# A Strassen-Winograd feed-forward: six open steps in place of five, earlier sums and a deeper prefetch for the down projection

## The chip, the cores and the metric

One core of one Trainium2 chip runs the whole kernel. The metric is device time in microseconds (us); each figure for a kernel is the median of several runs, and the range of the runs stands beside it.

## What is computed

One decoder layer on 1024 tokens of width 1024, all in float32. Two attention groups run first; the change does not touch them. Then come the output projection with a residual and a layer norm, a SwiGLU feed-forward with a second norm, and a gated embedding with a third. Cut to what matters:

```python
mix = jnp.concatenate([o_nsa, o_mla], axis=-1) @ w_out[i]
x = _layer_norm(ALPHA * x + mix, ln1_g[i], ln1_b[i])
gu = x @ w_up[i]
ffn = (jax.nn.silu(gu[..., :D_FF]) * gu[..., D_FF:]) @ w_down[i]
x = _layer_norm(ALPHA * x + ffn, ln2_g[i], ln2_b[i])
```

D_FF is 2816, which is 22 tiles of 128.

## The kernel before

**Numbers.** A float32 operand is split into a high half in fp32r (`hi`, L103 to L107, mostly on ACT) and the rest (`lo`, L109 to L113, mostly on DVE). A product is then three matmuls (`mm3`, L120: high by high, high by low, low by high), so the low half of the stationary operand is first wanted by the third matmul, L124.

**Output projection.** The loop over the eight token blocks `tb` (L1193 on) runs `out_proj` (48 matmuls, residual, statistics of the norm), a scaling on ACT (L1213), and one turn later `x1_done` (gain on DVE, L914; bias on DVE, L918; a copy to DRAM, L1191) and `tr_x1` (eight transposes on PE, L989, copied out by ACT, L996). `t_sums` forms the Winograd combinations of the transposed activations and `put` splits them (L1017 on ACT, L1019 on DVE, four small instructions for two blocks).

**Gate and up.** Gate and up are computed with Winograd's seven products per step `i`, one step for each of the 22 tiles. `seq` lists the (step, product) pairs; `k` is the place in it. A product is twelve matmuls. The first products of a step, 1 and 2, need only the gate weights and two combinations that are ready early; the other five need sums of weights (`u_sum`, four POOL instructions, L1041 to L1045) and the later combinations. So the first `SKEW` steps are opened: their products 1 and 2 all come first in `seq` (ten products with `SKEW` at 5), and the rest follows. `u_split` splits weights; `"g"` is the gate half, `"s12"` and `"s34"` are the sums. `u_evac` takes results out of PSUM one product later (L1085 on ACT, L1090 on DVE, then Silu on ACT, L1091). `at_pos` hangs each of these jobs on a place `k`, and every engine runs its instructions in the order in which they were written: an instruction that waits holds up all that is behind it on its engine. SP issues all DMAs, in order too.

**Down.** `h_sums` (POOL) forms combinations of the hidden tile and stores them to DRAM; `units` are the 77 down products of twelve matmuls, each with one operand pair that `d_load` reads back (256 KB of hidden, 256 KB of weights) and `d_split` splits two units ahead. `d_load` runs four units ahead, because the tag `kk` has four buffers. At units 2 and 13 four residual blocks each (`x1d`, 512 KB) are loaded (L1340).

**Buffers.** `slot()` hands out 43 buffers of 4 KB per partition (tag `b`), `kslot()` four (tag `kk`), `hslot()` twelve of half the size (tag `h`).

Of the kernel before, what the change touches and what calls it, by code (L numbers as in the profile page):

```python
# [37 lines left out]
SKEW = 5  # L38
# [29 lines left out]
def body(tc, sb, dr, A, out, dbg, stop):  # L68
# [978 lines left out]
    def u_split(i, what):  # L1047
        if i >= NF:
            return
        if what == "u":  # L1050
            t = slot(F32R, T)
            h, l = t[:, :512], t[:, 512:]
            hi_lo(h, l, RAW[i][1][:, 512:])
            WP7[i, 4] = h, l
            return
        x = {"g": lambda: RAW[("g", i) if i < SKEW else i], "s12": lambda: SS[i, 0], "s34": lambda: SS[i, 1]}[what]()
        x = x[0] if what == "g" and i >= SKEW else x
        ps = {"g": (1, 2), "s12": (5, 6), "s34": (7, 3)}[what]
        h, l = slot(F32R, T), slot(F32R, T)
        hi_lo(h, l, x)  # L1060
        for n, c in zip(ps, (0, 512)):
            WP7[i, n] = h[:, c:c + 512], l[:, c:c + 512]
# [19 lines left out]
    def u_evac(i, n):  # L1082
        if n in (1, 6, 5):
            t = CO[i, n] = hslot()
            act.activation(t, BK[i, "x"], AF.Copy)  # L1085
            if n == 5:
                dve.tensor_add(t, t, BK[i, "z"])
        elif n == 2:
            t = CO[i, 1]
            dve.tensor_add(t, t, BK.pop((i, "y")))  # L1090
            act.activation(t, t, AF.Silu)  # L1091
        elif n == 3:
            t = hslot()
            act.activation(t, BK.pop((i, "x")), AF.Silu)
            h = CO.pop((i, 5))
            dve.tensor_mul(h, h, t)
            keep_h(i, 1, h)
        elif n == 4:
            h = CO.pop((i, 6))
            dve.tensor_add(h, h, BK.pop((i, "z")))  # L1100
            dve.tensor_mul(h, h, CO.pop((i, 1)))
            keep_h(i, 0, h)
# [7 lines left out]

    def h_sums(m):
        a11, a21, a12, a22 = HA.pop((2 * m, 0)), HA.pop((2 * m, 1)), HA.pop((2 * m + 1, 0)), HA.pop((2 * m + 1, 1))
        s1, s2 = hslot(), hslot()
# [46 lines left out]
    for i in range(NF):  # L1160
# [4 lines left out]
        at_pos(first - 6 if i else 1, u_sum, i, 0)  # L1165
        at_pos(first - 5 if i else 1, u_sum, i, 1)
# [13 lines left out]
    for k, nm, tbs in ((0, "t2", (6,)), (0, "t3", (4, 5)), (2, "t2", (7,)), (3, "t3", (6, 7)), (4, "t1", (4, 5)),  # L1180
                       (5, "t1", (6, 7)), (7, "22", (4, 5, 6, 7)), (10, "t4", (4, 5)), (11, "t4", (6, 7))):
        for tb in tbs:
            at_pos(k, put, tb, nm)
# [12 lines left out]
    for tb in range(NB):  # L1196
# [4 lines left out]
        if tb in (6, 7):  # L1201
            g_fetch(tb - 6)
        if tb:
            x1_done(tb - 1)
        if tb == 7:
            u_split(0, "g")
            u_split(1, "g")
            g_fetch(2)
            g_fetch(3)
        nrm = out_proj(tb)  # L1210
        if tb:
            tr_x1(tb - 1)
        act.activation(acc[tb], acc[tb], AF.Identity, scale=nrm[0], bias=nrm[1])  # L1213
        if 1 <= tb <= 4:
            put(tb - 1, "11")
            put(tb - 1, "21")
        elif tb:
            t_sums(tb - 1)
    WO = None
    u_fetch(0)  # L1220
    put(4, "t2")
    put(5, "t2")
# [9 lines left out]
    RW, UN = {}, {}  # L1232

    def d_load(k):
        if k < len(units):
            n, m = units[k]
            t = RW[k] = kslot(T, F32)
# [14 lines left out]
    for k, (i, n) in enumerate(seq):  # L1252
# [8 lines left out]
        if k in (1, 3, 5):  # L1261
            u_split(k // 2 + 2, "g")
        if k == 1:
            g_fetch(4)
        jobs(k)
        last = i, n
        if len(seq) - 6 <= k < len(seq) - 2:
            d_load(k - len(seq) + 6)
# [52 lines left out]
    XB, YB = {}, {}  # L1321
    for k, (n, m) in enumerate(units):
# [8 lines left out]
        d_load(k + 4)  # L1331
# [5 lines left out]
        if k in (2, 13):  # L1337
            for tb in range(k // 11 * 4, k // 11 * 4 + 4):
                acc[tb] = slot(n=D)
                nc.sync.dma_start(acc[tb], x1d[tb])  # L1340
# [155 lines left out]
```

## Time and profile before

| | |
|---|---|
| median of 3 runs | 1463.13 us (1462.27 to 1465.5) |
| the profiled execution | 1464.8 us, of it span 1463.0 us |
| PE busy | 1409.4 us, 96% of the span |
| PE weight loads busy | 1179.3 us, 81% |
| DVE busy | 1010.7 us, 69% |
| ACT busy | 709.9 us, 49% |
| POOL busy | 591.3 us, 40% |
| DMA | 159.85 MB, 109 GB/s on average |
| mean granted PE clock | 0.989 |

PE is the engine that does nearly all of the time, and its idle time sits in few places. The output projection ends, and gate and up begin, at about 677 us of the span; the down projection begins at about 1120 us. Matmuls of a run overlap in the records, so a record of 0.39 us in a run of equal matmuls stands for a step of less than that from start to start; losses are therefore better counted from starts than from the busy share.

### The profile page before, as it was taken

The page shows a single profiled execution, that of the slowest core. Times are in us where ns is not written, and L with a number is a line of the kernel's source. Part 1 is how long each engine was busy: PE and PEld are TensorE (multiplying, and loading weights), DVE is VectorE, ACT ScalarE, POOL GpSimd, SP SyncE. Part 2 cuts the span into 40 slices and gives each one's busy share as a digit, 9 for nine tenths or more (in the row PEclk, how much of TensorE's full clock was granted, in tenths as well). Part 3 has the DMA queues.
Part 4 walks back from the last instruction along what each step waited for, and adds up shares of the span by engine and source line. Part 5 has one row for each costly group of instructions (what it writes and reads, how often), then busy time and mean ns, then how long its engine had stood idle before and what let it go on. Part 6 is the DMA issues. An engine that isn't in the chain of part 4 may idle for free. (4 is left out here: it accounts for less than half of the span.)

```text
span 1463.0 us, 20518 instructions
## 1 busy us (share of the span) xinstructions
PE 1409.4 (96%) x7082; PEld 1179.3 (81%) x7082; DVE 1010.7 (69%) x1923; ACT 709.9 (49%) x1447; POOL 591.3 (40%) x570
## 2 busy tenths in 40 slices
PE   8999899999989999998899999999999999999997
PEld 8987778888768887887688788888877788888886
DVE  5367589999988998578755555555554565686775
ACT  3323499888888888233532333333232343333221
POOL 1321165545443338013366866666682011121332
PEclk9999999999999999999999999999999999999999
DMA  7031000000000014123145444444454887662001
GB/s 274 16 100 52 26 1 23 2 1 15 2 15 1 1 44 158 58 87 123 65 166 183 165 151 163 166 166 165 167 193 148 291 295 240 242 212 76 29 30 58
DMA packets 66488, 159.85 MB, mean 109 GB/s; under 512 B 8016, under 2 KB 8656, under 8 KB 66384
## 3 DMA queue, kind: packets, MB, share of 16 engines
q1 hardware_dynamic: 66384, 158.54, 31.2%
q8 instruction: 56, 0.92, 0.3%
q14 instruction: 48, 0.39, 0.1%
HBM read 118.40 MB, written 40.11 MB: 108 GB/s over the span
## 5 line engine op out<-in xcount | busy, mean ns | idle before, releaser
L122 PE MATMUL p<-b 128*128 128x512 f32 (+3 forms) x1524 | 585.1, 384 | 15.3 <-ACT b L105 10.3
L124 PE MATMUL p<-b 128*128 128x512 f32 (+3 forms) x1524 | 583.9, 383 | 3.3 <-DVE b L111 3.1
L123 PE MATMUL p<-b 128*128 128x512 f32 (+3 forms) x1524 | 581.9, 382 | 1.5 <-DVE b L111 1.5
L122 PEld LDWEIGHTS p<-b 128*128 128x128 f32 x1524 | 288.3, 189 | 70.9 <-ACT b L105 12.2
L124 PEld LDWEIGHTS p<-b 128*128 128x128 f32 x1524 | 288.2, 189 | 62.1 <-DVE b L111 8.8
L123 PEld LDWEIGHTS p<-b 128*128 128x128 f32 x1524 | 288.4, 189 | 53.5 <-DVE b L111 2.4
L111 DVE TENSOR_TENSOR b<-b 128x1024 fp32r<-128x1024 f32 (+4 forms) x162 | 204.0, 1277 | 173.4 <-ACT b L105 134.4
L111 DVE TENSOR_TENSOR h<-p,h 128x512 fp32r<-128x512 f32 (+1 forms) x244 | 148.8, 627 | 12.0 <-ACT h L105 10.8
L532 ACT ACTIVATE b<-b,st 128x640 f32<-128x640 f32 (+7 forms) x192 | 142.8, 744 | 9.3 <-DVE st L481 7.1
L481 DVE CUSTOM_DVE_ANT_0 b<-s,b 128x640 f32<-128x640 f32 (+7 forms) x192 | 137.4, 716 | 10.4 <-PE s L486 6.8
L105 ACT ACTIVATE h<-p 128x512 fp32r<-128x512 f32 (+1 forms) x244 | 131.9, 550 | 26.0 <-PE p L591 22.6
L107 POOL TENSOR_SCALAR b<-b 128x1024 fp32r<-128x1024 f32 (+3 forms) x45 | 50.9, 1135 | 211.0 <-DMA b<-in_pT 64.1
L591 PE MATMUL p<-ident,b 128*128 128x128 f32 x816 | 129.3, 275 | 5.7 <-DVE b L732 1.9
L537 POOL TENSOR_SCALAR b<-b,st,gate 128x640 f32<-128x640 f32 (+7 forms) x128 | 101.0, 790 | 78.6 <-DVE st L579 42.4
L105 ACT ACTIVATE b<-kk 128x1024 fp32r<-128x1024 f32 x77 | 80.8, 1059 | 104.0 <-DMA kk<-in_wdown 52.9
L111 DVE TENSOR_TENSOR b<-kk,b 128x1024 fp32r<-128x1024 f32 x77 | 95.5, 1262 | 48.7 <-ACT b L105 47.6
L105 ACT ACTIVATE b<-b 128x1024 fp32r<-128x1024 f32 (+2 forms) x124 | 105.1, 858 | 42.3 <-POOL b L1045 15.2
L1085 ACT ACTIVATE h<-p 128x512 f32<-128x512 f32 x66 | 39.2, 594 | 174.2 <-PE p L124 174.2
L591 PEld LDWEIGHTS p<-ident,b 128*128 128x128 f32 x816 | 99.8, 141 | 25.9 <-POOL b L537 4.2
L486 PE MATMUL s<-b 128*128 128x320 f32 (+10 forms) x480 | 105.2, 339 | 4.1 <-DVE st L579 1.7
L607 PE MATMUL p<-h,b 128*128 128x512 f32 x228 | 103.9, 456 | 1.1 <-DVE h L111 0.9
L486 PEld LDWEIGHTS s<-b 96*128 96x128 f32 (+1 forms) x480 | 80.8, 190 | 21.9 <-issue 5.8
(178 smaller groups left out, 1702.1 us busy)
## 6 DMA issues: line engine op xcount, KB each, us to landing
b<-in_wup SPq DMA_DIRECT2D x49, 512.0 KB, 4.9
hd<-h SPq DMA_DIRECT2D x77, 256.0 KB, 2.1
kk<-hd SPq DMA_DIRECT2D x77, 256.0 KB, 4.3
b<-in_wdown SPq DMA_DIRECT2D x22, 512.0 KB, 4.6
td<-b SPq DMA_DIRECT2D x44, 256.0 KB, 2.7
kk<-td SPq DMA_DIRECT2D x44, 256.0 KB, 4.7
kk<-in_wdown SPq DMA_DIRECT2D x33, 256.0 KB, 5.0
b<-in_wT SPq DMA_DIRECT2D x8, 512.0 KB, 3.9
```

Of the source, the lines that this page charges most:

```text
L105: act.activation(h, x, AF.Copy)
L107: pool.tensor_scalar(h, x, 1.0, 1.0, op0=OP.mult, op1=OP.mult)
L111: dve.tensor_sub(l, x, f(h))
L122: pe.matmul(ps, ah, bh, start=start, stop=False, skip_group_check=more)
L123: pe.matmul(ps, ah, bl, start=False, stop=False, skip_group_check=more)
L124: pe.matmul(ps, al, bh, start=False, stop=stop, skip_group_check=more)
L481: dve.tensor_tensor_reduce(out=W, in0=ps, in1=bias, op0=OP.add, op1=OP.min, scale=scale, scalar=LOWEST, accum_out=m)
L486: pe.matmul(ps, q, k[:, c0:c1], start=i == 0, stop=i == len(terms) - 1)
L532: act.activation(w, w, AF.Exp, bias=self.low[:, m:m + 1], scale=-1.0, accum_out=self.sum[:, m:m + 1])
L537: pool.tensor_scalar(w, w, self.inv[:, m:m + 1], self.gates[m], op0=OP.mult, op1=OP.mult)
L591: pe.transpose(pt[:rows, i * 128:i * 128 + 128], u.WH if col < 0 else u.W[:, col:col + rows], ident)
L607: pe.matmul(ch.bank[:, c], v, th, start=start, stop=False)
```

## The change

`SKEW` becomes 6, so twelve products open gate and up. The weights of step 0 are fetched with turn 6 of the output projection and summed in turn 7, ahead of its matmuls; the gate halves of the other open steps come after. The last block's `t_sums` of block 6, the split of step 1 and two `put`s now stand ahead of the last scaling. The Silu of the open steps leaves `u_evac` and is issued at `k` = 3, 5, 7 and so on. The `put`s are spread over later places in smaller pieces. `h_sums` takes its two sums from one `kk` buffer for the first ten pairs. In the down projection the first eight loads are issued within the last ten products of gate and up, odd ones in slots, up to unit 29; the residual blocks are loaded one at a time.

```diff
--- before.py
+++ after.py
@@ -35,7 +35,7 @@
 SLOTS = 43
 HALVES = 12
 DPAIRS = 11
-SKEW = 5
+SKEW = 6
 PVLAG = 2
 CDMA = 1
 LATK = (1, 1)
@@ -1053,8 +1053,8 @@
             hi_lo(h, l, RAW[i][1][:, 512:])
             WP7[i, 4] = h, l
             return
-        x = {"g": lambda: RAW[("g", i) if i < SKEW else i], "s12": lambda: SS[i, 0], "s34": lambda: SS[i, 1]}[what]()
-        x = x[0] if what == "g" and i >= SKEW else x
+        x = {"g": lambda: RAW[("g", i) if 0 < i < SKEW else i], "s12": lambda: SS[i, 0], "s34": lambda: SS[i, 1]}[what]()
+        x = x[0] if what == "g" and not 0 < i < SKEW else x
         ps = {"g": (1, 2), "s12": (5, 6), "s34": (7, 3)}[what]
         h, l = slot(F32R, T), slot(F32R, T)
         hi_lo(h, l, x)
@@ -1088,7 +1088,8 @@
         elif n == 2:
             t = CO[i, 1]
             dve.tensor_add(t, t, BK.pop((i, "y")))
-            act.activation(t, t, AF.Silu)
+            if i >= SKEW:
+                act.activation(t, t, AF.Silu)
         elif n == 3:
             t = hslot()
             act.activation(t, BK.pop((i, "x")), AF.Silu)
@@ -1108,9 +1109,15 @@
         if n:
             nc.sync.dma_start(hd[i // 2][n - 1], h)
 
+    def hpair(m):
+        if m == DPAIRS - 1:
+            return hslot(), hslot()
+        s = kslot(T, F32)
+        return s[:, :512], s[:, 512:]
+
     def h_sums(m):
         a11, a21, a12, a22 = HA.pop((2 * m, 0)), HA.pop((2 * m, 1)), HA.pop((2 * m + 1, 0)), HA.pop((2 * m + 1, 1))
-        s1, s2 = hslot(), hslot()
+        s1, s2 = hpair(m)
         pool.tensor_tensor(s1, a21, a22, op=OP.add)
         nc.sync.dma_start(hd[m][4], s1)
         pool.tensor_tensor(s2, s1, a11, op=OP.subtract)
@@ -1162,8 +1169,9 @@
         first = min(s12, s34)
         if i >= SKEW:
             at_pos(pos[i, 1] - 2, u_split, i, "g")
-        at_pos(first - 6 if i else 1, u_sum, i, 0)
-        at_pos(first - 5 if i else 1, u_sum, i, 1)
+        if i:
+            at_pos(first - 6, u_sum, i, 0)
+            at_pos(first - 5, u_sum, i, 1)
         at_pos(first - 4, u_split, i, "u")
         at_pos(s34 - 2, u_split, i, "s34")
         at_pos(s12 - 2, u_split, i, "s12")
@@ -1177,8 +1185,9 @@
             k = min(pos[i, 4] + 1, len(seq) - 36 + 2 * m)
             at_pos(k - 5, d_fetch, m)
             at_pos(k, d_sums, m)
-    for k, nm, tbs in ((0, "t2", (6,)), (0, "t3", (4, 5)), (2, "t2", (7,)), (3, "t3", (6, 7)), (4, "t1", (4, 5)),
-                       (5, "t1", (6, 7)), (7, "22", (4, 5, 6, 7)), (10, "t4", (4, 5)), (11, "t4", (6, 7))):
+    for k, nm, tbs in ((0, "t2", (6,)), (2, "t2", (7,)), (3, "t3", (4,)), (4, "t3", (5, 6)), (5, "t3", (7,)),
+                       (6, "t1", (4, 5)), (8, "t1", (6, 7)), (10, "22", (4, 5)), (11, "22", (6, 7)),
+                       (12, "t4", (4, 5)), (13, "t4", (6, 7))):
         for tb in tbs:
             at_pos(k, put, tb, nm)
 
@@ -1198,28 +1207,32 @@
             out_load(tb + 2)
         if tb + 1 < NB:
             out_split(tb + 1)
-        if tb in (6, 7):
-            g_fetch(tb - 6)
+        if tb == 6:
+            u_fetch(0)
         if tb:
             x1_done(tb - 1)
         if tb == 7:
+            u_sum(0, 0)
+            u_sum(0, 1)
             u_split(0, "g")
-            u_split(1, "g")
-            g_fetch(2)
-            g_fetch(3)
+            g_fetch(1)
         nrm = out_proj(tb)
         if tb:
             tr_x1(tb - 1)
+        if tb == NB - 1:
+            t_sums(tb - 1)
+            u_split(1, "g")
+            put(4, "t2")
+            put(5, "t2")
         act.activation(acc[tb], acc[tb], AF.Identity, scale=nrm[0], bias=nrm[1])
         if 1 <= tb <= 4:
             put(tb - 1, "11")
             put(tb - 1, "21")
-        elif tb:
+        elif 0 < tb < NB - 1:
             t_sums(tb - 1)
     WO = None
-    u_fetch(0)
-    put(4, "t2")
-    put(5, "t2")
+    for i in range(2, SKEW):
+        g_fetch(i)
     if stop == 3:
         for tb in range(NB):
             dump(f"X1{tb}", acc[tb])
@@ -1230,11 +1243,12 @@
     ORDER = (1, 2, 6, 5, 3, 7, 4)
     units = [(n, m) for n in ORDER for m in range(DPAIRS)]
     RW, UN = {}, {}
+    DEEP = 30
 
     def d_load(k):
         if k < len(units):
             n, m = units[k]
-            t = RW[k] = kslot(T, F32)
+            t = RW[k] = slot(n=T) if k % 2 and k < DEEP else kslot(T, F32)
             nc.sync.dma_start(t[:, :512], hd[m][n - 1])
             if n in (1, 2, 3):
                 src = A["wdown"][2 * m + (n > 1)][:, (n == 3) * 512:(n == 3) * 512 + 512]
@@ -1258,14 +1272,14 @@
         elif k == 2:
             tr_x1(NB - 1)
             t_sums(NB - 1)
-        if k in (1, 3, 5):
+        if k % 2 and k // 2 + 2 < SKEW:
             u_split(k // 2 + 2, "g")
-        if k == 1:
-            g_fetch(4)
         jobs(k)
+        if 3 <= k < 3 + 2 * SKEW and k % 2:
+            act.activation(CO[(k - 3) // 2, 1], CO[(k - 3) // 2, 1], AF.Silu)
         last = i, n
-        if len(seq) - 6 <= k < len(seq) - 2:
-            d_load(k - len(seq) + 6)
+        if len(seq) - 10 <= k < len(seq) - 2:
+            d_load(k - len(seq) + 10)
         if k >= len(seq) - 2:
             d_split(k - len(seq) + 2)
     u_evac(*last)
@@ -1319,6 +1333,7 @@
         for what, d in ((0, 0), (1, 2), (2, 3)):
             more.setdefault(base + 5 * tb + d, []).append((ln2_step, tb, what))
     XB, YB = {}, {}
+    XAT = (2, 4, 6, 8, 13, 15, 17, 19)
     for k, (n, m) in enumerate(units):
         if m == 0:
             if n in (1, 2, 7):
@@ -1328,16 +1343,16 @@
                 else:
                     YB = B
             B = YB if n in (2, 7, 4) else XB
-        d_load(k + 4)
+        d_load(k + 8) if k + 8 < DEEP else k + 4 >= DEEP and d_load(k + 4)
         d_split(k + 2)
         h, l = UN.pop(k)
         for b in range(4):
             c = slice(b * 128, b * 128 + 128)
             mm3(B[b], h[:, c], l[:, c], h[:, 512:], l[:, 512:], n in (1, 2, 7) and m == 0, m == DPAIRS - 1, n not in (1, 2, 7))
-        if k in (2, 13):
-            for tb in range(k // 11 * 4, k // 11 * 4 + 4):
-                acc[tb] = slot(n=D)
-                nc.sync.dma_start(acc[tb], x1d[tb])
+        if k in XAT:
+            tb = XAT.index(k)
+            acc[tb] = slot(n=D)
+            nc.sync.dma_start(acc[tb], x1d[tb])
         if k == 5 * DPAIRS - 3:
             ln2 = load_ln(2)
         for fn, *args in more.pop(k, []):
```

How the order moves, engine by engine. First POOL, at turn 7 of the output projection (L901 and L967 belong to a block's norm, L1006 and L1007 to `t_sums`, L1041 to L1045 to `u_sum`); a piece of the difference:

```order
 L1006 TENSOR_TENSOR kk<-kk 128x512
 L1007 TENSOR_TENSOR b<-b,h 128x512
+L1041 TENSOR_TENSOR b<-b 128x512
+L1042 TENSOR_TENSOR b<-b 128x512
+L1044 TENSOR_TENSOR b<-b 128x512
+L1045 TENSOR_TENSOR b<-b 128x512
 L901 TENSOR_TENSOR ls<-ls,half 128x1
 L967 TENSOR_SCALAR ls<-ls 128x1
```

The four sums of step 0 moved from behind the last `t_sums` of that loop to ahead of the norm of block 7.

Second ACT, from the transposed block 6 (L996) on, in the kernel before (L1213 is the last scaling, L1017 `put`, L1085 a result copied from PSUM, L105 the split of a gate half, L1091 Silu):

```order
L996 ACTIVATE kk<-p 128x512 x2
L1213 ACTIVATE b<-b,ls 128x1024
L1017 ACTIVATE b<-h 128x2x128 x6
L1017 ACTIVATE b<-kk 128x2x128 x4
L1085 ACTIVATE h<-p 128x512
L105 ACTIVATE b<-b 128x1024
L1091 ACT_TABLE_LOAD
L1091 ACTIVATE h<-h 128x512
L996 ACTIVATE kk<-p 128x512 x2
```

and the same place in the changed kernel (L1227 is the last scaling there):

```order
L996 ACTIVATE kk<-p 128x512 x2
L105 ACTIVATE b<-b 128x1024
L1017 ACTIVATE b<-h 128x2x128 x4
L1227 ACTIVATE b<-b,ls 128x1024
L1017 ACTIVATE b<-h 128x2x128 x2
L1085 ACTIVATE h<-p 128x512
L105 ACTIVATE b<-b 128x1024
L996 ACTIVATE kk<-p 128x512 x2
```

The first Silu is gone from between the copies; a gate split and four `put`s went ahead of the scaling.

Third SP, at the end of gate and up in the changed kernel, with buffer numbers (`hd_n_...` are the hidden combinations in DRAM; L1252 and L1257 are `d_load`, L1110 and L1122 to L1128 are stores of the last pair):

```order
+L1252 DMA b<-hd_1_7304 128x512
+L1257 DMA b<-in_wdown 128x512
+L1110 DMA hd_1_7353<-h 128x512
+L1252 DMA kk<-hd_1_7311 128x512
+L1257 DMA kk<-in_wdown 128x512
+L1252 DMA b<-hd_1_7318 128x512
+L1257 DMA b<-in_wdown 128x512
+L1252 DMA kk<-hd_1_7325 128x512
+L1257 DMA kk<-in_wdown 128x512
+L1252 DMA b<-hd_1_7332 128x512
+L1257 DMA b<-in_wdown 128x512
+L1110 DMA hd_4_7356<-h 128x512
```

The loads of units 3 to 7 now stand ahead of the stores of the last pair; before, only units 0 to 3 did.

## Rows read from the trace of the kernel before

**Rows 1.** Windows of 20 us (start:end length, busy of each engine with count, PEclk, DMA share, GB/s)

```profile
680.00:700.00 20.00, 14.29 (x61) 11.76 (x60) 16.58 (x22) 11.16 (x23) 8.38 (x7) 0.83 0.44 149
...
1140.00:1160.00 20.00, 16.97 (x67) 13.37 (x66) 11.35 (x12) 10.60 (x10) 0.00 (x0) 0.91 0.70 248
```

**Rows 2.** Timeline, PE, start of gate and up (start, duration, group, [idle before <-releaser])

```profile
691.17 1.94 PE L989 MATMUL p<-ident,b 128*128 128x128 f32 x8 [5.71 <-DVE b L918]
...
695.17 0.39 PE L122 MATMUL p<-b 128*128 128x512 f32 x1
...
707.18 0.39 PE L124 MATMUL p<-b 128*128 128x512 f32 x1
710.58 0.50 PE L122 MATMUL p<-b 128*128 128x512 f32 x1 [3.01 <-ACT b L105]
...
715.36 0.40 PE L123 MATMUL p<-b 128*128 128x512 f32 x1
...
720.76 0.50 PE L122 MATMUL p<-b 128*128 128x512 f32 x1 [2.02 <-ACT b L105]
...
725.61 0.40 PE L123 MATMUL p<-b 128*128 128x512 f32 x1
```

**Rows 3.** Timeline, PE, start of the down projection

```profile
1130.26 0.39 PE L124 MATMUL p<-b 128*128 128x512 f32 x1
1132.50 0.49 PE L122 MATMUL p<-b 128*128 128x512 f32 x1 [1.85 <-ACT b L105]
...
1144.26 0.50 PE L122 MATMUL p<-b 128*128 128x512 f32 x1 [2.27 <-ACT b L105]
...
1148.96 0.40 PE L122 MATMUL p<-b 128*128 128x512 f32 x1
```

**Rows 4.** Timeline, DVE, around the first two stops

```profile
675.73 0.69 DVE L964 SCALAR_TENSOR_TENSOR b<-b,p 128x512 f32<-128x512 f32 x1 [0.58 <-PE p L124]
...
682.10 5.46 DVE L1019 TENSOR_TENSOR b<-h,b 128x256 fp32r<-128x256 f32 x4 [1.75 <-ACT b L1017]
687.49 2.28 DVE L914 TENSOR_TENSOR b<-b 128x1024 f32<-128x1024 f32 x1
689.80 1.23 DVE L918 TENSOR_TENSOR b<-b 128x1024 f32<-128x1024 f32 x1
690.94 0.75 DVE L1019 TENSOR_TENSOR b<-h,b 128x256 fp32r<-128x256 f32 x2
...
700.81 5.81 DVE L1019 TENSOR_TENSOR b<-kk,b 128x256 fp32r<-128x256 f32 x4
```

**Rows 5.** Timeline, ACT, around the first two stops

```profile
680.52 1.24 ACT L1213 ACTIVATE b<-b,ls 128x1024 f32<-128x1024 f32 x1 [2.58 <-POOL ls L967]
...
697.47 0.73 ACT L1017 ACTIVATE b<-h 128x256 fp32r<-128x256 f32 x2 [1.07 <-DVE h L1005]
698.11 0.57 ACT L1085 ACTIVATE h<-p 128x512 f32<-128x512 f32 x1
...
707.24 0.63 ACT L1091 ACTIVATE h<-h 128x512 f32<-128x512 f32 x1 [6.39 <-DVE h L1090]
```

**Rows 6.** Timeline, POOL, last blocks of the output projection

```profile
669.24 1.29 POOL L1007 TENSOR_TENSOR b<-b,h 128x512 f32<-128x512 f32 x1
679.04 0.93 POOL L901 TENSOR_TENSOR ls<-ls,half 128x1 f32<-128x1 f32 x1 [8.51 <-DVE ls L900]
```

**Rows 7.** Timeline, SP's DMA queue, start of the down projection

```profile
1127.24 0.32 SPq L1121 DMA_DIRECT2D hd<-h  x1
...
1130.52 1.96 SPq L1340 DMA_DIRECT2D b<-x1d  x4
```

**Rows 8.** DMA issues of 661 to 670 us (x count, KB, median us to landing)

```profile
b<-in_wup SPq DMA_DIRECT2D x1, 512.0 KB, 4.4
```

**Rows 9.** DMA issues of 1100 to 1175 us

```profile
kk<-in_wdown SPq DMA_DIRECT2D x22, 256.0 KB, 5.0
b<-x1d SPq DMA_DIRECT2D x8, 512.0 KB, 6.9
```

## The prediction

> **What bounds the kernel now.** I read the windows first. PE is busy in all of a 20 us window from 740 to 1120 us but for some tenths, and again after 1160. It is not around 700 us, where the window from 680 has 14.29 us of it, nor around 1140, where the window has 16.97; the granted clock there is 0.83 and 0.91 [rows 1], which is 2.4 GHz for most of the window and 1.2 GHz for the rest. So PE bounds the kernel, and the change can win only what PE loses at these two places. The reader is to see that both lie where a stage begins.
>
> Second, PE's own timeline, to count the losses from starts. From 695.17 to 707.18 there are 53 steps without a stop: 0.2266 us a matmul, 2.72 a product of twelve [rows 2]. Four stops stand against that:
> - Stop A: the transposes of the last block start at 691.17, after 5.71 us idle, released by DVE's L918 [rows 2].
> - Stop B: from 707.18 to 715.36 are 11 steps, 2.49 us of work in 8.18, a loss of 5.69. It begins with 3.01 us idle until ACT's split L105 [rows 2].
> - Stop C: from 715.36 to 725.61 are 24 steps, 5.44 in 10.25, a loss of 4.81, behind ACT's L105 again [rows 2].
> - Stop E: from 1130.26 to 1148.96 are 46 steps, 10.43 in 18.70, a loss of 8.27, in two stops that wait for ACT's split of an operand [rows 3]. Some 5.1 of it belongs to the second one.
>
> Third, the timelines of the engines that release these stops. At A, DVE took 5.46 us for four small subtractions and 2.28 for L914, where two of the small ones alone take 0.75 and L918, of L914's size, takes 1.23 [rows 4]. In those 5.46 us POOL ran its sums, L1041 to L1045, one after the other. At B it is the same: 5.81 for four while POOL summed step 1 [rows 4]; DVE's L1090 came late, and ACT stood 6.39 us at a Silu that wanted it [rows 5], with the split that PE needed behind it. At E, SP issued the loads of units 4 on only behind the last store of a hidden combination, at 1127.24 [rows 7].
>
> **The two engines' turns.** The rows show a price of one POOL sum, 1.3 us or somewhat more, for each DVE instruction that reads two SBUF operands beside it (5.46 and 5.81 over four) [rows 4]; a DVE instruction that reads PSUM, such as L964, I take as free of it. The Trainium skill (SBUF — State Buffer, "SBUF: two separate sides") says that the two share one port pair, held by whichever started first for a whole instruction. That rule speaks against moving sums beside the norm of block 6; the trace agrees with the whole-instruction wait. What it leaves open, who gets the next turn, is the second rival.
>
> **The change, part by part.** The number of matmuls, sums, copies and loaded bytes stays; what moves is their order. One Silu per open step is later, and its table load with it.
>
> *Stop A.* POOL is free at 670.53 (669.24 + 1.29) [rows 6] and then runs the four sums. Their weights were fetched two turns of the output projection earlier, and one such load lands in 4.4 us [rows 8]. DVE's L918 of block 6, and the split of step 0, take turns with them: L918 ends near 674.1, the split near 676.5. PE wants the first at 676.2 and the second's low half at 677.4, so neither stops it. L964 of the last block, at 675.73 before [rows 4], starts about 0.9 later, so POOL's L901, 679.04 before [rows 6], starts at 679.95, and the scaling that began at 680.52 [rows 5] runs from 681.45 to 682.7. DVE meanwhile does step 1's split from 681.4 to 682.6 and four small subtractions in turns with only two POOL instructions of 1.29: done at 686.55. Then L914 and L918 at 1.15 each (689.80 to 690.94 [rows 4]), no sum beside them: 688.85, transposes at 688.95 in place of 691.17. **Gain 2.2.** PE still idles 3.5 us and I leave the half clock behind it as it is. Bounds: with no turn lost at all the transposes start when PE gets there, a gain of 5.7; if the gate load of step 1, now issued after the store of block 6, landed 6.9 us after its issue at 674.6, as in a crowd of loads [rows 9], it would still be there at 681.5, ahead of 682.6, so I see no loss below 0 except by the second rival.
>
> *Stop B.* It goes if step 4's split is ready. PE would start that product at 705.2 (707.41 less 2.2). On ACT, after the copies and sums of the last block at about 692.9, come eight small copies at 0.37, two results at 0.57, one Silu at 0.63 [rows 5], two splits at no more than the 1.24 of the scaling [rows 5] and the table load, by estimate no longer than these: 8.5 us, so step 4's high half is there by 701.4. On DVE, from 688.85: ten small subtractions at 0.37 (0.75 for two), four of `t_sums` and two L1090 at 0.7 (L964's 0.69), three splits at 1.15 [rows 4], together 11.4 us, 700.25. The four sums of step 1 land on POOL at about 695 and cost at most four turns of 1.3: 705.45; I take 705.0, the last turn being partly over. The low half is needed by the third matmul, 705.65. So both bounds hold PE harmless: **gain 5.69**, with 0.2 us to spare at the worse one.
>
> *Stop C.* The first product on sums, (0,6), is now two products further back: it starts at 716.1. DVE's list up to its split (ten small subtractions, three L1090, a half split at 0.7, two splits) adds 8.8 us to 705.0, so 713.8; on ACT the same jobs are shorter, and the sums themselves were done in the output projection. **Gain 4.81.** The next tight place is (1,6) at 724.3: twelve small subtractions, one L1090, two splits and a half put its low half at 721.9, two turns with the sums of step 2 at 724.5, against a need at 724.75. Lower bound of B and C together: all of it comes back, 0.
>
> *Stop E.* Units 0 to 7 are issued in the last ten products. They take 8 x 2.72 = 21.8 us from 1119.6, counted in the old time. Unit 8 is issued behind the same last store as unit 4 was, 1127.24 [rows 7], lands 5.0 later [rows 9] and needs two instructions of at most 1.24 to be split [rows 4, 5]: 1134.7, against a start at 1141.4. From then on loads run eight units ahead. The four residual blocks that went out at once at 1130.52 [rows 7] and took 6.9 us each to land [rows 9] now go out one by one. **Gain 8.27**; lower bound 3.2, if the second stop stays.
>
> *At no cost:* the 4 KB slots for odd loads come out of what the gate weights of late steps leave free; SP waits for them only on products that lie 1 to 8 units back. The two sums of `h_sums` in a `kk` buffer wait for a store one pair, 38 us, earlier. The later Silus stand behind work that is ready; first wanted by product (0,4), 30 us on. Late next: the remaining 3.5 us of stop A, and small stops of some tenths in the steady steps, which stay.
>
> **Sum.** 2.2 + 5.69 + 4.81 + 8.27 = 20.97 us. Against the profiled execution of 1464.8 that is 1443.8; this execution lies 1.67 above the median of 1463.13, so **1442.1 us**.
>
> **The rivals.**
> 1. *The opening is only half cleared.* DVE has 0.6 and 0.2 us to spare at products 8 and 15. If turns with POOL cost 1.45 (5.81 / 4) and fall ahead of these products, one stop of B's or C's kind comes back with the half clock behind it, 5.25 us: 1447.4. For it: DVE has no gap from 688 to 728 in my list. Against: ACT no longer stands behind a Silu.
> 2. *POOL keeps the turn.* If the sums of step 0 run in a row, L918 waits for all four, to 676.9, and ends at 678.1; PE's transposes of block 6 start 1.9 late and those of the last block at 690.5. A then gives 0.7: 1443.6. Against: the four in 5.46 us [rows 4], one between each two sums. The Trainium skill's rule of the first to start (same page and section) leaves it possible.
> 3. *The prefetch clears one stop of two.* The loads of units 8 on still come too late, and 5.1 us stay: 1447.2. Against: six us to spare.
> 4. *Nothing moves*: B and C come back behind other waits and E's second stop stays, 2.2 + 3.2 gained less a stop of 5: 1463.
> 5. *Slower.* Each residual block, now alone ahead of an operand on SP's queue, stops PE as the four did at the second stop, 5.1 us, eight times: 40.8 less 20.97 is 19.8 lost, 1483. It decides when an operand lands less than 2.5 us before its unit. Against: the lead is 21.8 us.
>
> **How the numbers follow.** Forecast 0.64, rivals 1 to 5 at 0.16, 0.07, 0.06, 0.04 and 0.03. A measurement of this kernel can tell about 0.2%, 2.9 us, from no change. The forecast's own range is 1437 (A gone whole with its slow clock) to 1445; the range reaches over rivals 1 to 3, and a little past them for two small returns: 1437 to 1451. Faster 0.93, same 0.04, slower 0.03.
>
> **What would show it.** The transposes of the last block behind an idle of about 3.5 us; no PE wait of over 1 us from 692 to 740; no stop in the first eight units of the down projection; POOL's first L1041 near 670.5, with L918 beside it at over 2 us. It is wrong if ACT's L105 or DVE's L111 releases a PE stop of over 2 us in the opening, or if units 8 to 20 of the down projection wait for a load.

## The result, and the profile after

The changed kernel takes 1445.26 us (median of four executions, 1444.45 to 1448.01) against 1464.06 for the kernel before in the same comparison: a ratio of 0.9876, 95% interval 0.9857 to 0.9894, or 18.8 us less. Four more executions later gave 1447.91 (1443.77 to 1449.13), ratio 0.988 (0.986 to 0.9899). The forecast was 21.0 less and 1442.1. The profiled execution took 1444.51, its span is 1442.7 and its PE clock 0.991; PE is busy for 1403.5 us, 97%.

In the changed kernel the last scaling is L1227 (L1213 before), the residual loads are L1355 (L1340) and the Silus of the open steps L1279 (L1091).

The time up to the first product of gate and up changes from execution to execution with nothing in the change to move it: that product starts at 677.01 us before, at 676.47 in this profile, and between 676.5 and 678.5 in all profiles below. The cleaner measure is the time from it to the end of the span: 786.0 before, 766.2 now, **19.8 less**.

The windows of the changed kernel (columns as in [rows 1]) show both places of [rows 1] and one that was not there:

```profile
680.00:700.00 20.00, 17.66 (x81) 14.19 (x80) 19.37 (x25) 14.44 (x31) 8.95 (x7) 1.00 0.43 153
700.00:720.00 20.00, 20.00 (x90) 16.55 (x89) 19.54 (x35) 16.37 (x38) 3.75 (x4) 1.00 0.17 54
760.00:780.00 20.00, 16.61 (x73) 13.51 (x72) 11.44 (x9) 4.81 (x7) 14.24 (x10) 0.98 0.50 155
780.00:800.00 20.00, 20.00 (x84) 16.40 (x83) 9.87 (x9) 5.94 (x9) 11.39 (x9) 0.94 0.70 266
1120.00:1140.00 20.00, 20.00 (x90) 16.57 (x89) 10.15 (x11) 10.16 (x10) 0.00 (x0) 1.00 1.04 387
```

PE is whole from 700 and whole in the down projection, but it lacks 3.4 us between 760 and 780, where the kernel before has it full:

```profile
760.00:780.00 20.00, 20.00 (x90) 16.58 (x89) 12.80 (x10) 7.42 (x10) 14.14 (x9) 1.00 0.47 171
```

PE's timeline of the changed kernel shows the same (it answers to [rows 2]):

```profile
687.51 1.07 PE L989 MATMUL p<-ident,b 128*128 128x128 f32 x8 [2.35 <-DVE b L918]
688.33 0.48 PE L122 MATMUL p<-b 128*128 128x512 f32 x1
...
775.73 0.39 PE L123 MATMUL p<-b 128*128 128x512 f32 x1
779.50 0.79 PE L124 MATMUL p<-b 128*128 128x512 f32 x1 [3.39 <-DVE b L111]
780.10 0.63 PE L122 MATMUL p<-b 128*128 128x512 f32 x1
...
782.59 0.40 PE L122 MATMUL p<-b 128*128 128x512 f32 x1
```

Stop A is down to 2.35 us idle and has no slow clock behind it. From 688.64 on no step is off the pitch until a **new stop at 779.50**, which costs 3.54 us and, with the half clock up to 782.59, 1.50 more. Counted from starts as the prediction did (all steps of over 0.245 us, what they have above 0.2266, with the eight transposes of a block as one step):

| PE loss, us | 679 to 740 | 740 to 810 | 810 to 1100 | 1100 to 1160 |
|---|---|---|---|---|
| before | 18.73 | 0.00 | 4.15 | 8.24 |
| changed | 3.40 | 5.05 | 3.09 | 0.00 |
| gain | 15.33 | -5.05 | 1.06 | 8.24 |

The gains add up to 19.6 of the 19.8.

Where the new stop comes from is read engine by engine, backwards, in the changed kernel. On DVE (first fence) the low half that PE wants, the split of step 5's sums `s12`, is the last of a row that begins only at 772.76. On ACT (second) that row waits for a split that stood 5.72 us for POOL's L1045. On POOL (third) step 5's sums began at 766.04, waiting for their load; its buffers had come free with the end of step 4's L1045 at 760.45 (758.71 + 1.74; SP issued the load at 760.47), and step 4's sums stood behind `d_sums` (from 740.50) and `h_sums`.

```profile
772.76 1.10 DVE L111 TENSOR_TENSOR b<-b 128x512 fp32r<-128x512 f32 x1 [4.34 <-ACT b L105]
773.78 1.77 DVE L1097 TENSOR_TENSOR h<-h 128x512 f32<-128x512 f32 x1
...
777.17 2.28 DVE L111 TENSOR_TENSOR b<-b 128x1024 fp32r<-128x1024 f32 x1
```

```profile
772.09 0.63 ACT L105 ACTIVATE b<-b 128x512 fp32r<-128x512 f32 x1 [5.72 <-POOL b L1045]
772.63 0.58 ACT L1095 ACTIVATE h<-p 128x512 f32<-128x512 f32 x1
773.11 1.05 ACT L105 ACTIVATE b<-b 128x1024 fp32r<-128x1024 f32 x1
```

```profile
740.50 1.67 POOL L1145 TENSOR_TENSOR b<-b 128x512 f32<-128x512 f32 x1 [3.24 <-DVE b L111]
...
753.08 2.27 POOL L1041 TENSOR_TENSOR b<-b 128x512 f32<-128x512 f32 x1
...
758.71 1.74 POOL L1045 TENSOR_TENSOR b<-b 128x512 f32<-128x512 f32 x1
766.04 1.30 POOL L1041 TENSOR_TENSOR b<-b 128x512 f32<-128x512 f32 x1 [5.60 <-DMA b<-in_wup]
```

### The profile page after: what moved, and what is told of

The parts are those of the page before. It is cut to its first block, busy times and chain, and to the rows that moved or that the text cites. A ratio compares the mean times of both kernels' runs of the same rounds, so it can differ in the third digit from the quotient of the medians.

```text
span 1442.7 us, 20481 instructions
## 1 busy us (share of the span) xinstructions
PE 1403.5 (97%) x7082; PEld 1176.7 (82%) x7082; DVE 1008.2 (70%) x1923; ACT 709.5 (49%) x1447; POOL 594.8 (41%) x570
## 5 line engine op out<-in xcount | busy, mean ns | idle before, releaser
L111 DVE TENSOR_TENSOR b<-b 128x1024 fp32r<-128x1024 f32 (+4 forms) x177 | 227.0, 1299 | 170.6 <-ACT b L105 129.3
L111 DVE TENSOR_TENSOR h<-p,h 128x512 fp32r<-128x512 f32 (+1 forms) x244 | 148.7, 627 | 11.5 <-ACT h L105 10.3
L105 ACT ACTIVATE b<-b 128x1024 fp32r<-128x1024 f32 (+2 forms) x139 | 121.0, 880 | 48.4 <-POOL b L1045 18.1
L105 ACT ACTIVATE h<-p 128x512 fp32r<-128x512 f32 (+1 forms) x244 | 131.9, 550 | 25.2 <-PE p L591 21.7
L1085 ACT ACTIVATE h<-p 128x512 f32<-128x512 f32 x66 | 39.2, 594 | 183.4 <-PE p L124 181.3
L105 ACT ACTIVATE b<-kk 128x1024 fp32r<-128x1024 f32 x62 | 65.2, 1059 | 86.4 <-DMA kk<-td 49.4
L901 POOL TENSOR_TENSOR ls<-ls,half 128x1 f32<-128x1 f32 x24 | 18.6, 774 | 177.4 <-DVE ls L900 177.4
```

The lines of the kernel that those rows point to most:

```text
L105: act.activation(h, x, AF.Copy)
L111: dve.tensor_sub(l, x, f(h))
```

## The experiments

All kernels are the changed one with the edit shown. "First to end" is from the first product of gate and up to the end of the profiled span; the losses are counted as above.

| kernel | median (range), us | ratio to before (95%) | first to end | 679-740 | 740-810 | 810-1100 | 1100-1160 |
|---|---|---|---|---|---|---|---|
| e1_u5_behind | 1448.03 (1445.28-1448.62) | 0.9881 (0.9865-0.9898) | 768.1 | 5.03 | 5.22 | 3.13 | 0 |
| e2_dsums_later | 1446.35 (1445.69-1446.57) | 0.9872 (0.9857-0.9888) | 767.5 | 4.99 | 4.66 | 3.16 | 0 |
| e3_silu_back | 1458.36 (1457.22-1459.39) | 0.9955 (0.9942-0.9968) | 778.9 | 14.25 | 6.71 | 3.14 | 0 |
| e4_puts_back | 1448.16 (1447.48-1450.14) | 0.9888 (0.9871-0.9904) | 768.2 | 5.00 | 5.26 | 3.23 | 0 |
| e5_sums_back | 1452.11 (1451.47-1455.67) | 0.992 (0.9907-0.9932) | 773.1 | 8.63 | 6.77 | 3.07 | 0 |
| e6_five_open | 1443.78 (1441.93-1445.15) | 0.9858 (0.9843-0.9872) | 764.2 | 4.97 | 0.96 | 3.48 | 0 |
| e7_shallow_loads | 1452.95 (1449.64-1454.94) | 0.9916 (0.9902-0.993) | 775.6 | 5.03 | 6.29 | 3.46 | 6.13 |
| e8_blocks_together | 1448.61 (1445.7-1449.64) | 0.9889 (0.9873-0.9904) | 766.6 | 4.98 | 3.77 | 3.13 | 0 |
| e9_changed_again | 1447.91 (1443.77-1449.13) | 0.988 (0.986-0.9899) | 769.9 | 5.00 | 7.01 | 3.28 | 0 |
| e10_no_dsums_open | 1443.39 (1443.14-1443.65) | 0.9858 (0.9843-0.9873) | 763.8 | 4.99 | 0.00 | 4.19 | 0 |
| e11_five_open_puts | 1442.81 (1442.37-1443.48) | 0.9854 (0.984-0.9869) | 763.2 | 3.50 | 1.18 | 3.67 | 0 |
| e12_all_three | 1442.28 (1441.29-1442.45) | 0.9849 (0.9834-0.9864) | 762.7 | 3.53 | 0.00 | 4.36 | 0 |

The changed kernel's own eight executions reach from 1443.77 to 1449.13, so medians of 1444 to 1449 do not differ from it by themselves; there the losses of the profile decide.

**The new stop, e1 and e2.**

```diff
-        at_pos(first - 4, u_split, i, "u")
+        at_pos(first + -1 if i == SKEW - 1 else first - 4, u_split, i, "u")
```

> Only the split of step 5's weight quarter (u_split 'u', step 5) moves, from place 31 to place 34, behind the split of its sums s12. Theory: the changed kernel's new stop at 779.5 us (3.39 idle, 5.0 us with its slow clock) comes from that split, which stands on ACT in front of a Silu and of s12 while it waits 5.72 us for POOL's sums of step 5; with it out of the way ACT's Silu of (3,3) and DVE's work behind it run about 5 us earlier, s12 is ready near 776 and the stop falls to 0.5 us or less: 1445.3 - 4.6 = 1440.7. Rival: POOL's sums themselves are the late ones and s12 waits for them anyway; then the stop stays at 3 us or more and the time at 1444 to 1446.

```diff
             k = min(pos[i, 4] + 1, len(seq) - 36 + 2 * m)
+            k += 3 if m == 0 else 0
```

> Only the first down sums (d_fetch and d_sums of pair 0) move three places later, from 18 and 23 to 21 and 26, so that POOL does step 4's sums ahead of them. Theory: the new stop begins on POOL, which at 740.5 to 753.1 did d_sums and h_sums of pair 0 before the sums of step 4 at 753.08, planned for 745; the loads of step 5 wait for the buffers of those sums, so step 5's sums began only at 766.04. Moved, step 5's sums end near 767 instead of 772.06 and the stop at 779.5 falls to 0.5 us or less: 1440.7. Rival: the stop is only the order on ACT and DVE, or the moved sums take turns with DVE at another place and stop PE there: 1444 to 1448.

In both the stop stayed: 3.50 us idle at 782.35 in e1, 2.77 at 762.16 in e2, one step earlier. DVE's timeline of e1, then of e2, shows why:

```profile
773.71 1.29 DVE L1102 TENSOR_TENSOR h<-h 128x512 f32<-128x512 f32 x1
780.02 3.95 DVE L111 TENSOR_TENSOR b<-b 128x1024 fp32r<-128x1024 f32 x2 [5.01 <-POOL b L1149]
```

```profile
759.84 2.87 DVE L111 TENSOR_TENSOR b<-b 128x1024 fp32r<-128x1024 f32 x2 [7.70 <-POOL b L1149]
```

The edit of e1 did what it should on ACT, but now the low half of `s12` was given a buffer that `d_sums` of pair 1 had to read first (L1149). In e2 step 4's splits waited for `d_sums` of pair 0 in the same way. My theory, one split in the wrong place, fell in e1. In e2 the rival held as to a stop at another place, though a buffer made it and not a turn with DVE. What is common to all three traces is that a split waits for a buffer which POOL's sums have still to free.

**The same, taken away at the source: e10.**

```diff
             k = min(pos[i, 4] + 1, len(seq) - 36 + 2 * m)
+            k = {0: pos[5, 4] + 8, 1: pos[7, 4] + 8}.get(m, k)
```

> The changed kernel with the down sums of pairs 0 and 1 taken out of the open steps altogether, to places behind steps 5 and 7, where a step has seven products of PE time instead of five. Theory: the stop near 780 is POOL's: in the open steps it has four sums a step, and four more of each of d_sums and h_sums every other step, for five products of PE time, and the splits wait for buffers that only its sums free. Without d_sums there, the stop is gone in whatever order the splits stand, 5 us: from the first product to the end 761.5 to 763.5, about 1441. Rival: there is another holder of the buffers, or the later places now stop PE instead: 765 to 768 and 1444 to 1447.

The stop is gone (0.00 from 740 to 810) and first to end is 763.8, 0.3 above the expected range. POOL's timeline of e10 (to compare with 753.08 to 766.04 above):

```profile
750.68 1.29 POOL L1041 TENSOR_TENSOR b<-b 128x512 f32<-128x512 f32 x1
...
754.56 1.30 POOL L1045 TENSOR_TENSOR b<-b 128x512 f32<-128x512 f32 x1
759.56 1.29 POOL L1041 TENSOR_TENSOR b<-b 128x512 f32<-128x512 f32 x1 [3.70 <-DMA b<-in_wup]
```

Without `d_sums` step 5's sums begin 6.5 us earlier though the first product was 0.8 later. The moved sums cost two stops of 0.7 us, at 822 and 861, hence 4.19 behind 810 in place of 3.1 to 3.5. The edit moves the loads of `d_sums` (`d_fetch`) too, and with them the buffers that these hold; POOL's time and those buffers were not taken away one by one.

**What cleared the opening: e3, e4, e6.**

```diff
-            if i >= SKEW:
-                act.activation(t, t, AF.Silu)
+            act.activation(t, t, AF.Silu)
...
-        if 3 <= k < 3 + 2 * SKEW and k % 2:
-            act.activation(CO[(k - 3) // 2, 1], CO[(k - 3) // 2, 1], AF.Silu)
```

> The Silus of the open steps go back to where they were, straight behind their DVE add. Theory: stop B and C did not end because of the later Silus; in the changed trace DVE's L1090 of steps 1, 2 come 8.0 and 14.4 us after the start of product 3 where before step 1's alone came 13.8 after it, so ACT would stand at a Silu for about 1 to 2 us at most and step 5's split still has over 2 us to spare: within 1 us of the changed kernel, 1444.5 to 1446.5. Rival (the prediction's argument against its first rival, that ACT no longer stands behind a Silu): a stop of B's kind comes back, 3 to 5 us, 1448 to 1450.

The rival was right and too small: 1458.36. The opening loses 14.25 us, 9.2 more than the 5.0 of the other kernels; the later stop, 6.71, lies within what it has in the other profiles (3.77 to 7.01). ACT's timeline of e3:

```profile
700.18 0.63 ACT L1091 ACTIVATE h<-h 128x512 f32<-128x512 f32 x1 [4.04 <-DVE h L1090]
...
706.03 0.63 ACT L1091 ACTIVATE h<-h 128x512 f32<-128x512 f32 x1 [1.95 <-DVE h L1090]
...
711.21 0.63 ACT L1091 ACTIVATE h<-h 128x512 f32<-128x512 f32 x1 [1.89 <-DVE h L1090]
...
725.30 0.63 ACT L1091 ACTIVATE h<-h 128x512 f32<-128x512 f32 x1 [4.26 <-DVE h L1090]
```

Each Silu waits for DVE's L1090; behind it stand ACT's copies and splits, and DVE's next instructions wait for those. A row of DVE's, then PE's stops in e3:

```profile
701.22 2.03 DVE L1019 TENSOR_TENSOR b<-kk,b 128x256 fp32r<-128x256 f32 x4 [1.07 <-ACT b L1017]
```

```profile
716.69 0.50 PE L122 MATMUL p<-b 128*128 128x512 f32 x1 [0.78 <-ACT b L105]
...
727.69 0.79 PE L122 MATMUL p<-b 128*128 128x512 f32 x1 [4.43 <-ACT h L1085]
```

The two engines take turns instead of running side by side, and both fall behind (DVE is busy for 13.80 us of the window from 700 to 720, where the changed kernel has 19.54), until PE stops 4.43 us for a result (L1085) that ACT has not yet taken out of PSUM. My mistake was to read how late L1090 was in a trace in which nothing held it up.

```diff
-    for k, nm, tbs in ((0, "t2", (6,)), (2, "t2", (7,)), (3, "t3", (4,)), (4, "t3", (5, 6)), (5, "t3", (7,)),
+    for k, nm, tbs in ((0, "t2", (6,)), (0, "t3", (4, 5)), (2, "t2", (7,)), (3, "t3", (6, 7)), (4, "t1", (4, 5)),
...
```

> The table of the puts goes back to that of the kernel before (larger pieces, earlier places), with six open steps and all else as changed. Theory: what cleared B was DVE's list: up to step 4's split at place 5 the old table puts three blocks more ahead of it, six small subtractions, 2.2 us alone and up to 4 in turns with POOL, where the changed trace has 0.2 us to spare; a stop of 2 to 4 us with a slow clock of about 1.5 comes back near 702: 1448.5 to 1451. Rival: the two more open products have slack enough, no stop: 1445.

No stop: 5.00 in the opening, as in the other kernels. With the slow clock behind stop A, which is there in e4, the spreading of the puts is worth nothing that can be measured. Without that clock it would be worth some tenths at most, by estimate: in e4 step 4's split ends at 704.62 for a matmul that starts at 706.14, and 1.6 us of that start come from the clock, so the split would be about 0.1 us late.

```diff
-SKEW = 6
+SKEW = 5
```

> SKEW is 5 again, everything else as changed. Theory: the sixth open step buys little in the opening now that ACT no longer stands behind a Silu (product (0,6) comes two places earlier; DVE's list has its sums' split ready within 0 to 1.5 us of the need), and it costs the stop near 780, because POOL and the 43 buffers fall behind over the open steps, one step fewer then: the stop near 780 is 1 us or less and the opening loses 0.5 to 2.5: 1441 to 1443. Rival (the prediction's reason for stop C): the first product on sums comes too early by a whole stop with its slow clock, 4.8 us, and the later stop stays: 1447 to 1450.

1443.78: the opening is as it was (4.97, nothing but stop A) and the stop near 780 is gone; the 0.96 left from 740 to 810 is mostly another one, of 0.57 us idle at 803.57. The opening is even better than the theory gave it (0.5 to 2.5 lost), and the sixth open step, which buys nothing there, costs the new stop. POOL's row of sums is there in e6 too. Its first sum of step 5, then the PE matmul that wants the low half of that step's `s12`:

```profile
763.01 1.29 POOL L1041 TENSOR_TENSOR b<-b 128x512 f32<-128x512 f32 x1 [5.76 <-DMA b<-in_wup]
```

```profile
783.64 0.39 PE L124 MATMUL p<-b 128*128 128x512 f32 x1
```

POOL does the same twelve sums in a row as in the changed kernel, here from 737.32 to 757.25, and step 5's sums wait as long for their load. But counted from the first product they begin 3.7 us earlier, and with five open steps `seq` has step 5's product (5,6) at place 37, not at 35: the sums begin 20.6 us ahead of the matmul that wants them, where the changed kernel has 9.9 (766.04 to 775.96, where that matmul would have started).

**Stop A and stop E, undone one by one: e5, e7, e8.**

```diff
-        if i:
-            at_pos(first - 6, u_sum, i, 0)
-            at_pos(first - 5, u_sum, i, 1)
+        at_pos(first - 6 if i else 1, u_sum, i, 0)
+        at_pos(first - 5 if i else 1, u_sum, i, 1)
...
-            u_sum(0, 0)
-            u_sum(0, 1)
```

> The four sums of step 0 go back to place 1 of gate and up; their weights are still fetched early. Theory: the early sums are what shortened stop A. Back, POOL runs them beside DVE's last puts and its norm of the last block, which took 5.46 and 2.28 us before and 2.52 and 1.21 after the change; the last transposes come 3 to 4 us later, PE idles about 6 us there and the slow clock follows: the part from the first product of gate and up to the end 3.5 to 5.5 us longer than the changed kernel's 766.2, a time of 1449 to 1451. Rival: it is the new order ahead of the last scaling (sums and puts first) that shortened A, and the place of the sums is worth under 1 us: 1445 to 1446.

PE idles 5.25 us before the last transposes, the opening loses 8.63, 3.6 more than with the sums early. First to end is 6.9 longer than in the first profile of the changed kernel, which is more than expected, and 3.2 longer than in the repeat (e9), whose stop near 780 is as long as the one here. The early sums shortened A; the rival falls.

```diff
-            t = RW[k] = slot(n=T) if k % 2 and k < DEEP else kslot(T, F32)
+            t = RW[k] = kslot(T, F32)
...
-        if len(seq) - 10 <= k < len(seq) - 2:
-            d_load(k - len(seq) + 10)
+        if len(seq) - 6 <= k < len(seq) - 2:
+            d_load(k - len(seq) + 6)
...
-        d_load(k + 8) if k + 8 < DEEP else k + 4 >= DEEP and d_load(k + 4)
+        d_load(k + 4)
```

> The loads of the down operands run four units ahead again in kk buffers alone, as before the change; the residual blocks are still loaded one at a time. Theory: both parts of stop E return only if the residual blocks' crowd was not the cause of the second one; I expect the first stop back, 3.2 us (the operand of unit 4 behind the last hidden store), and the second gone: 1448.5. Rival: the lead alone decided, both stops come back, 8.3 us: 1453.5.

```diff
-        if k in XAT:
-            tb = XAT.index(k)
-            acc[tb] = slot(n=D)
-            nc.sync.dma_start(acc[tb], x1d[tb])
+        if k in (2, 13):
+            for tb in range(k // 11 * 4, k // 11 * 4 + 4):
...
```

> The deep loads stay, the residual blocks go out four at once again, at units 2 and 13. Theory: with eight units of lead, 21.8 us, four blocks (2 MB, about 5.4 us at the 387 GB/s of 1120 to 1140 us) delay operands that are not wanted yet: no stop, 1445 to 1446. Rival: the crowd delays operands by 7 us or more and eats the lead, a stop of 2 to 5 us near unit 8 to 12 of the down projection: 1447 to 1450.

In e7 one stop came back. PE's timeline of e7 at the start of the down projection, to hold against [rows 3]:

```profile
1125.02 0.50 PE L122 MATMUL p<-b 128*128 128x512 f32 x1 [2.04 <-ACT b L105]
1126.28 0.79 PE L123 MATMUL p<-b 128*128 128x512 f32 x1 [0.76 <-DVE b L111]
```

These two steps lose 3.23, as the theory had it, and the slow clock behind them, which the first stop of [rows 3] did not have, 2.9: together 6.13. The second stop did not return. The median is 4.5 above the 1448.5 expected, 2.9 of it this clock. In e8 no stop came back; its median is above the range expected, but its executions spread as the changed kernel's own do, and nothing in its profile answers to the edit. So loading the residual blocks one by one clears the second stop by itself, the deep loads clear both, and with them the blocks' order does not matter.

**The changed kernel again, e9,** with no edit.

> The changed kernel once more, beside the others of this call. Its profile had no slow clock behind the last block's transposes after 2.35 us idle, while six of the eight kernels run since, with 2.3 to 2.4 us idle at the same place, show it (1.6 us). Theory: that is chance of a single execution; the time from the first product of gate and up to the end is 766 to 768.5 us, the median 1445 to 1448, and the stop near 780 is there again with 3.3 to 3.7 idle. Rival: the changed kernel keeps full clock there for a reason of its own: 766.2 again.

The slow clock behind stop A is there this time (5.00 in place of 3.40), and the stop near 780 is longer, 3.96 us idle and 7.01 in all. The theory was right on stop A; on first to end it gave up to 768.5 and I measured 769.9, since the later stop itself varies.

**Towards a faster kernel, e11 and e12.** e11 is e6 with this:

```diff
-            put(4, "t2")
-            put(5, "t2")
...
             x1_done(NB - 1)
+            put(4, "t2")
+            put(5, "t2")
```

> Five open steps (as the kernel with SKEW 5 and all else changed, 1443.8), and the two puts of t2 for blocks 4 and 5 moved from ahead of the last scaling to behind the last block's norm. Theory: the four small copies on ACT (1.32 us) stand ahead of the scaling and the four small subtractions on DVE (2.52) ahead of the norm's two instructions, for a product that comes ten places later; without them L914 starts near 682.4 in the changed kernel's time, L918 ends by 684.9 to 685.9, PE idles 0 to 0.8 us instead of 2.35 and keeps its clock: 2.5 to 4 us less, 1440 to 1441.5. Rival: the puts then delay the next splits in DVE's list and a stop of 2 us or more comes in the opening: 1443 to 1446.

Stop A falls to 1.02 us idle with full clock, but a stop of 0.74 comes at 703.64, in the opening, at the product of stop B: 3.50 lost there against 4.97. The gain over e6 is 1.0 us by medians, whose ranges overlap, and by first to end (764.2 to 763.2), in place of 2.5 to 4; theory and rival each held in part. e12 is e11 with the edit of e10.

> The kernel with five open steps and the puts behind the norm, and also the down sums of pairs 0 and 1 moved out of the open steps. Theory: the last stop of 0.6 us there (0.85 with the steps near it) goes too and nothing comes for it: 0.5 to 1 us below the kernel without this move, 1439 to 1441. Rival: with five open steps POOL had caught up anyway and the moved sums meet DVE in a full step, two or three stops of 0.5 us: 1441 to 1443.

1442.28: the difference to e11, 0.5, is as expected, and the level above the range since e11 was. All four executions of e12 (up to 1442.45) lie below all eight of the changed kernel (from 1443.77). PE's timeline and one window of e12:

```profile
687.29 1.06 PE L989 MATMUL p<-ident,b 128*128 128x128 f32 x8 [1.00 <-DVE b L918]
...
703.33 0.50 PE L124 MATMUL p<-b 128*128 128x512 f32 x1 [0.72 <-DVE b L111]
```

```profile
760.00:780.00 20.00, 20.00 (x90) 16.55 (x89) 10.61 (x10) 7.29 (x10) 8.16 (x7) 1.00 0.39 132
```

## Why the prediction was right, and where not

**Stop A, forecast 2.2, measured 4.8 in this profile and 3.2 in the repeat.** The mechanism was right; the term was mis-sized. DVE's timeline of the changed kernel:

```profile
668.79 2.27 DVE L914 TENSOR_TENSOR b<-b 128x1024 f32<-128x1024 f32 x1 [1.45 <-ACT b L1227]
671.09 2.20 DVE L918 TENSOR_TENSOR b<-b 128x1024 f32<-128x1024 f32 x1
673.21 2.30 DVE L111 TENSOR_TENSOR b<-b 128x1024 fp32r<-128x1024 f32 x1
675.44 0.68 DVE L964 SCALAR_TENSOR_TENSOR b<-b,p 128x512 f32<-128x512 f32 x1
...
682.44 2.52 DVE L1019 TENSOR_TENSOR b<-h,b 128x256 fp32r<-128x256 f32 x4
684.89 1.21 DVE L914 TENSOR_TENSOR b<-b 128x1024 f32<-128x1024 f32 x1
```

POOL's timeline beside it:

```profile
669.94 2.27 POOL L1041 TENSOR_TENSOR b<-b 128x512 f32<-128x512 f32 x1
672.28 2.15 POOL L1042 TENSOR_TENSOR b<-b 128x512 f32<-128x512 f32 x1
674.40 2.26 POOL L1044 TENSOR_TENSOR b<-b 128x512 f32<-128x512 f32 x1
676.62 1.29 POOL L1045 TENSOR_TENSOR b<-b 128x512 f32<-128x512 f32 x1
```

DVE's first three rows are the foreseen turns with POOL's sums, about 2.2 each, and they made L964 0.25 us later against the first product (1.03 ahead of it; before, 1.28, from 675.73 [rows 4] to 677.01), where I had taken 0.9. The four small subtractions took 2.52 and not 5.46 [rows 4], and ended 8.42 us after the first product where my list said 9.54. So 1.1 us of PE's idle time went that I had left in, 2.35 in place of 3.5. The slow clock, which I left in as well, is missing in the first profile and there in the repeat; that is the difference of 4.8 and 3.2.

These rows also bear on the rule from the Trainium skill (SBUF — State Buffer, "SBUF: two separate sides"): the trace agrees that the wait is for a whole instruction, and that L964, which reads PSUM, runs in 0.68 us while POOL is in a sum. Whose turn is next, on which the second rival rested, the rows answer: one instruction each, with POOL's first sum at 669.94 (near 670.5 was named) and L918 beside it at 2.20 (over 2 was named).

**Stops B and C, forecast 5.69 and 4.81, measured both in full.** No PE wait of over 1 us was left from 692 to 740, as written. The margin was about right, too: step 4's low half ended at 702.18 (700.96 + 1.22) and the matmul that reads it started at 702.51, 0.3 us to spare where the prediction had 0.2:

```profile
700.96 1.22 DVE L111 TENSOR_TENSOR b<-b 128x1024 fp32r<-128x1024 f32 x1
```

```profile
702.51 0.39 PE L124 MATMUL p<-b 128*128 128x512 f32 x1
```

What failed is the credit. For C the step was "The first product on sums, (0,6), is now two products further back"; e6 takes those two products away and C does not return. The later Silus stood under "at no cost", and as an argument against the first rival; e3 shows that they are worth 9.2 us in the opening, in size nearly all of B and C. The place is C's and the products behind it: in e3 PE stops at (0,6) and, for longer, two products on, while B's product, (4,1), is still clear. What cleared B itself is open: none of e3 to e6 alone brings it back, and only e11 and e12, with five open steps and two puts moved, have a stop there (0.74 and 0.72 us idle).

**Stop E, forecast 8.27, measured 8.24.** Right: no stop in the first units nor later. Its lower bound left the second stop; e7, with the residual blocks' order alone, has it the other way round: the first stays and the second is gone. The deep loads (e8) clear both.

**The new stop, in no term: -5.05 here, -7.0 in the repeat.** The step that failed is "Late next: the remaining 3.5 us of stop A, and small stops of some tenths in the steady steps, which stay", which names nothing between the opening and the steady steps. I looked for the next late thing in the opening and the down projection, and not at POOL between them. Its load can be worked out from rows: an open step is five products, 13.6 us; POOL has four sums for it and eight more every second step, eight on average, at 1.3 to 1.7 us 10.4 to 13.6 us. By this estimate it has little slack or none, but the trace does not show it falling behind from step to step: from 700 to 740 it is busy for 13.38 of 40 us. What the trace shows is one stretch: from 740.50 to 760.45 POOL runs twelve sums without a pause, and only then the load of step 5 gets its buffers. That the `d_sums` of pairs 0 and 1 in this stretch are the source is shown by e10, though not whether by POOL's time or by the buffers of their loads; that the sixth step makes the difference, by e6. There POOL has the same row, but step 5's sums begin 20.6 us ahead of the matmul that wants them, not 9.9. The stop also bears on the sign of being wrong: DVE's L111 did release a PE stop of over 2 us, at 779.50, while the open steps still ran, but behind the stretch from 692 to 740 in which the prediction looked for it.

**The sum.** 20.97 forecast from four gains; measured 15.33 and 8.24, and 1.06 in the small stops, less 5.05. A's gain being larger hid half of the new stop; that the sum came out so near is in part luck. The time lies within the forecast's own range up to 1445 but for 0.3 us, and the repeat at 1447.91 inside the wide one. None of the rivals as described took place; the first, one stop with its half clock, 5.25 us and 1447.4, came nearest in size, but its stop was to come in the opening, and the new one stands some 60 us later and behind other waits.

## What to carry to other kernels

When an opening is tightened, follow the helper engine's instructions over the whole stretch until the steady state, and ask of each step when its results are wanted: here POOL had eight sums on average for five products, the sixth open step wanted step 5's sums two products earlier, and the stop came 91 us behind stop A. Where two in-order engines pass small results to and fro, move the instruction that waits, not the ones that are waited for: one Silu per step, put back, cost 9.2 us in the opening, more than any other part that was put back by itself (3.6 for the early sums, nothing measurable for the puts and the sixth step). When a stop follows the buffers, reordering one of its victims hands the wait to the next; take the work that holds them out of that stretch.

## What the hardware showed that I had not expected

A PE idle time of 2.3 to 2.4 us at the same place let the granted clock fall in nine profiles of ten (all but e5, e11 and e12, whose idle time there is another; seven of them before e9, not six as its expectation says), and not in the first: the window from 680 to 700 has 1.00 there and 0.91 in the repeat, where the opening lost 1.6 us more. After 1.0 us idle (e11, e12) it stayed at 2.4 GHz. One kernel's stop is also not one number: the stop near 780 was 3.39 us idle in the one profile of the changed kernel and 3.96 in the other, 5.05 and 7.01 with what follows.
